# A PLE gate whose multiply moves from GpSimd in the gate stage to VectorE in the down stage (transformer block, one core)

## The chip, the core and the metric

The kernel runs on one NeuronCore of one Trainium2 chip. The metric is the device time of one execution in microseconds (us). Three executions of the kernel before took 978.75, 979.18 and 979.24 us; the median, 979.18 us, is the time that the change is measured against. The hardware profiler took one further execution of the same program; all rows below come from it.

## The reference, cut to what matters

One block on 512 tokens of width 1024, all in float32: a layer norm, a wide projection with a spatial gate and a gated recurrence, a merge, an output product `w_o` and a second layer norm that gives `h1`. The change touches what follows:

```python
hid = silu(h1 @ w_ffn_gate) * (h1 @ w_ffn_up)          # width 2816
ffn = hid @ w_ffn_down
ple = sigmoid(h1 @ w_ple_gate + b_ple_gate) * (p @ w_ple)
out = layer_norm(ALPHA * h1 + ffn + ple, ln2_g, ln2_b)
```

## The kernel before, in words

**Precision and units.** TensorE multiplies in a reduced 32-bit type, so each float32 operand is split into a high and a low part and each product is three matmuls (high x high, high x low, low x high). A unit of weights is 128 x 1024 elements (512 KB): it is loaded into a `raw` buffer by a DMA that SP issues, ScalarE casts the high part (`wh`, line 62), VectorE subtracts for the low part (`wl`, line 65). `wh` and `wl` have five buffers each, so these splits run ahead of TensorE by at most five units.

**Seven products.** The PLE gate and the up stage use a Strassen-like scheme (`strassen`, line 161): a product of 2 x 2 blocks takes seven block products instead of eight, named X, W, Z, Y, Z2, Y2 and Y3 after the accumulation they add to. It needs sums of weight blocks: t1 and t2 are added by GpSimd (line 181), t3 and t4 by accumulating DMAs that GpSimd issues (line 179); t4 is added into the buffer of t2 and read by the last product, Y3. The sums of activations come from `combine` (line 133).

**The stages around the change.** The product `p @ w_ple` is made at the very start and put into DRAM (`ple_dram`, line 412). Much later, after the second layer norm, comes the PLE gate (`pg_prod`, `pg_evac`, lines 884 to 923). For each of the four output quadrants (c11, c12, c22, c21; 256 tokens x 512 columns each) `pg_evac` loads the PLE product of that quadrant into `pl` (line 910, SP), adds the two partial results on VectorE (line 916), takes the sigmoid on ScalarE (line 918), multiplies it by `pl` on GpSimd (line 919) and stores the result back to `ple_dram` (line 920, SP). The up stage (`up`, line 931) follows: eleven groups of 256 columns, each a seven-product scheme over the gate and up weights, ending in `hid`. The down stage (lines 972 to 1031) first scales the residual in `r1` (`g1`, line 988), loads the gated PLE (`gp`, line 987), adds the bias `b1` to it (line 989) and adds the two (line 990). Then come eleven pairs of down units, `wd`, each with a split of the activations (`hidh`, `hidl`) and 48 matmuls; the last two pairs form a tail that ends one token tile after the other, and the residual is added as each accumulator is read (lines 1016 and 1024).

**What sets the order.** The code is written in Tile. A planner in the compiler simulates a timeline and from it fixes the order of the instructions on every engine's queue, in which earlier program text has priority among what is ready. On the chip each queue (TensorE, VectorE, ScalarE, GpSimd, SP) runs strictly in that order: an instruction that waits holds up everything behind it on its queue, DMA issues included. So a change in one place can move instructions elsewhere. Buffers of a pool with the same tag are reused in turn, and a load into one waits for the last reader of its previous content.

Of the kernel before, what the change touches and what calls it, by code (L numbers as in the profile page):

```python
# [8 lines left out]
F32 = mybir.dt.float32  # L9
# [3 lines left out]
ALU = mybir.AluOpType  # L13

P = 128
D = 1024
KT = D // P
T = 512
TT = T // P
# [13 lines left out]
def block_kernel(  # L33
# [7 lines left out]
    nc = tc.nc  # L41
    V, S, G, PE = nc.vector, nc.scalar, nc.gpsimd, nc.tensor
# [11 lines left out]
    dram = ctx.enter_context(tc.tile_pool(name="dram", bufs=1, space=bass.MemoryType.DRAM))  # L54

    def ps_tile(name):
        return psum.tile([P, 2, 512], F32, tag="ps", name=name)
# [22 lines left out]
    def unit_b(w, k0, c0, name, **kw):  # L80
        return load_unit(
            w[k0 * P:(k0 + 2) * P, c0:c0 + 512].rearrange("(k p) c -> p k c", p=P), 2, 512, name, **kw)
# [169 lines left out]
    def load_bc(pool, vec, name, n=D, tag=None, bufs=1):  # L252
        t = pool.tile([P, n], F32, tag=tag or name, name=name, bufs=bufs)
        nc.sync.dma_start(t, row_bc(vec, n))
        return t
# [20 lines left out]
    def ln_aggr(st, mr):  # L276
        V.bn_aggr(out=mr, in_=st.rearrange("p a b -> p (a b)"))
        rsqrt(mr[:, 1:2], mr[:, 1:2], LN_EPS)
# [21 lines left out]
    hh = hpool.tile([P, KT, T], F32R, name="hh")  # L300
    hl = hpool.tile([P, KT, T], F32R, name="hl")
    ple_dram = dram.tile([P, TT, D], F32, name="ple_dram")


    hgb_cm = tc.tile_pool(name="hgb", bufs=1, side="right")
# [400 lines left out]
    for c in range(2):  # L706
# [5 lines left out]
        for a in range(2):  # L712
            o = vn[:, 2 * a:2 * a + 2, 512 * c:512 * c + 512]
            V.tensor_tensor(out=o, in0=pss[a],
                            in1=b_v[:, 512 * c:512 * c + 512].unsqueeze(1).broadcast_to([P, 2, 512]), op=ALU.add)
# [56 lines left out]
    with tc.tile_pool(name="mg", bufs=1) as mp:  # L772
# [15 lines left out]
        for m in range(KT // 2):  # L788
            residual(m)
            res = []  # L790
            for nm, off, w, ah, al in (("a", OGA, wa, yah, yal), ("b", OGB, wb, ybh, ybl)):
                psg = ps_tile(f"ps_mg{nm}{m}")
                gemm_a(psg, win, off + 256 * m, hh, hl, f"g{nm}{m}")
                sg = mp.tile([P, 2, T], F32, tag="sg", name=f"sg{nm}{m}", bufs=3)
# [18 lines left out]
    with tc.tile_pool(name="l1", bufs=1) as lp:  # L813
        bpg = load_bc(lp, b_ple_gate[0], "bpg")
        h1f = lp.tile([P, KT, T], F32, name="h1f")
        acc = [ps_tile(f"ps_wo{t}") for t in range(TT)]

        def wo_mm(t, kp, us):
            for c in range(2):
                h, l = us[c]  # L820
                for k in range(2):
                    kk = 2 * kp + k
                    mm_b(acc[t][:, c, :], t, mgh, mgl, kk, h, l, k, kk == 0, kk == KT - 1)

        def wo_tail(t):
            for c in range(2):
                for kp, us in tails:
                    h, l = us[c]
                    for k in range(2):
                        kk = 2 * kp + k  # L830
                        mm_b(acc[t][:, c, :], t, mgh, mgl, kk, h, l, k, kk == 0, kk == KT - 1)

        for kp in range(2):
            us = [unit_b(wo, 2 * kp, 512 * c, f"wo{kp}_{c}") for c in range(2)]
            for t in range(TT):
                wo_mm(t, kp, us)
        tails = [(kp, [unit_b(wo, 2 * kp, 512 * c, f"wo{kp}_{c}") for c in range(2)]) for kp in (2, 3)]

        def turn(t):
            ps = ps_tile(f"ps_h1_{t}")  # L840
            psv = ps.rearrange("p a (b c) -> p (a b) c", c=P)
            for k in range(KT):
                PE.transpose(psv[:, k, :], r1[:, t, k * P:(k + 1) * P], ident)
            f = h1f[:, :, t * P:(t + 1) * P]
            for k in range(KT):
                S.activation(f[:, k, :], psv[:, k, :], AF.Identity, scale=vecT[:, 104 + k:105 + k],
                             bias=vecT[:, 112 + k:113 + k])
            if t < 2:
                ts = slice(t * P, t * P + P)
                for n, fs in (("11", f[:, 0:4, :]), ("12", f[:, 4:8, :])):  # L850
                    split(comb[n][0][:, :, ts], comb[n][1][:, :, ts], fs)
            else:
                combine(comb, cpool, h1f, slice((t - 2) * P, (t - 1) * P))

        def norm1(t):

            r = r1[:, t, :]
            st = lp.tile([P, 2, 6], F32, tag="lnst1", name=f"lnst1_{t}", bufs=2)
            for c in range(2):
                o = r[:, 512 * c:512 * c + 512]  # L860
                V.tensor_tensor(out=o, in0=acc[t][:, c, :], in1=o, op=ALU.add)
                V.bn_stats(out=st[:, c, :], in_=o)
            mr = lp.tile([P, 3], F32, tag="mr1", name=f"mr1_{t}", bufs=2)
            ln_aggr(st, mr[:, 0:2])
            V.scalar_tensor_tensor(out=mr[:, 2:3], in0=mr[:, 0:1], scalar=-1.0, in1=mr[:, 1:2],
                                   op0=ALU.mult, op1=ALU.mult)
            S.activation(r, r, AF.Identity, scale=mr[:, 1:2], bias=mr[:, 2:3])

        for t in range(TT):
            wo_tail(t)  # L870
            if t > 1:
                turn(t - 2)
            with tc.high_priority(offset=300):
                norm1(t)
        mgpool_cm.__exit__(None, None, None)
        yapool_cm.__exit__(None, None, None)
        cpool_cm = tc.tile_pool(name="comb", bufs=1, side="right")
        cpool = cpool_cm.__enter__()
        comb.update({n: tuple(cpool.tile([P, 4, HT], F32R, name=f"c{n}{z}") for z in "hl") for n in COMB[2:]})
        with tc.tile_pool(name="pg", bufs=1, side="right") as pp:  # L880
            pch = {}
            pmid = {}

            def pg_prod(chain, units, n, first, last):
                if first:
                    pch[chain] = ps_tile(f"ps_pg{chain}")
                for t in range(2):
                    product_b(pch[chain], units, comb[n], first, last, t)
                    if n in ("11", "12") and t == 1:
                        turn(2 if n == "11" else 3)  # L890

            def pg_mid(n, x, y, op):
                pmid[n] = pp.tile([P, 2, 512], F32, name=f"pg_{n}")
                for t in range(2):
                    V.tensor_tensor(out=pmid[n][:, t, :], in0=x[:, t, :], in1=y[:, t, :], op=op)

            def pg_evac(n):
                bias = [bpg[:, 512 * c:512 * c + 512].unsqueeze(1).broadcast_to([P, 2, 512]) for c in range(2)]
                if n == "p1":

                    pg_mid("p1", pch["X"], bias[0], ALU.add)
                    pg_mid("p1c", pch["X"], bias[1], ALU.subtract)
                elif n in ("y6", "z5"):
                    pg_mid(n, pch[n[0].upper()], pmid["p1c"], ALU.subtract)
                else:
                    i, j = int(n[1]) - 1, int(n[2]) - 1
                    cs = slice(512 * j, 512 * j + 512)
                    sg = pp.tile([P, 2, 512], F32, tag="sgp", name=f"sgp{i}{j}", bufs=2)
                    pl = pp.tile([P, 2, 512], F32, tag="pl", name=f"pl{i}{j}", bufs=2)
                    nc.sync.dma_start(pl, ple_dram[:, 2 * i:2 * i + 2, cs])  # L910
                    chain, add = {"c11": ("W", "p1"), "c22": ("Y", "z5"), "c12": ("Z", "y6"), "c21": ("Y", "p1")}[n]
                    x, y = pch[chain], pmid[add]
                    if n == "c21":
                        x, y = y, x
                    for t in range(2):
                        V.tensor_tensor(out=sg[:, t, :], in0=x[:, t, :], in1=y[:, t, :],
                                        op=ALU.subtract if n == "c21" else ALU.add)
                    S.activation(sg, sg, AF.Sigmoid)
                    G.tensor_tensor(out=sg, in0=sg, in1=pl, op=ALU.mult)
                    nc.sync.dma_start(ple_dram[:, 2 * i:2 * i + 2, cs], sg)  # L920

            strassen(wx, [[src_b(wpg, 4 * a, 4, 512 * b) for b in range(2)] for a in range(2)], "pg",
                     "X W Z Y Z2 Y2 Y3", pg_prod, pg_evac)


# [46 lines left out]
    with tc.tile_pool(name="fin", bufs=1) as lp:  # L972
# [8 lines left out]
        b1 = load_bc(lp, ln1_b[0], "b1", tag="lng", bufs=2)  # L981
        S.activation(g1, g1, AF.Copy, scale=ALPHA)
        S.activation(b1, b1, AF.Copy, scale=ALPHA)
        for t in range(TT):
            r = r1[:, t, :]
            gp = lp.tile([P, D], F32, tag="gp", name=f"gp{t}", bufs=2)
            nc.sync.dma_start(gp, ple_dram[:, t, :])
            V.tensor_tensor(out=r, in0=r, in1=g1, op=ALU.mult)
            V.tensor_tensor(out=gp, in0=gp, in1=b1, op=ALU.add)
            V.tensor_tensor(out=r, in0=r, in1=gp, op=ALU.add)  # L990
        g2 = load_bc(lp, ln2_g[0], "g2", tag="lng", bufs=2)
        b2 = load_bc(lp, ln2_b[0], "b2", tag="lng", bufs=2)
        acc = [ps_tile(f"ps_d{t}") for t in range(TT)]
# [15 lines left out]
        for t in range(TT):  # L1009
            r = r1[:, t, :]  # L1010
# [17 lines left out]
            for c in range(2):  # L1028
                cs = slice(512 * c, 512 * c + 512)
# [35 lines left out]
```

## Time and profile before

| what | value |
|---|---|
| median of three executions | 979.18 us |
| the profiled execution, its time | 981.31 us |
| its span, first to last instruction | 979.6 us |
| TensorE matmuls busy | 939.3 us, 96% |
| VectorE busy | 609.7 us, 62% |
| ScalarE busy | 360.6 us, 37% |
| GpSimd busy | 247.4 us, 25% |
| mean granted TensorE clock | 0.99 of full speed |

PE is TensorE, PEld its weight load, DVE is VectorE, ACT ScalarE, POOL GpSimd, SP the engine that issues most DMAs. Times in rows are microseconds from the start of the span unless marked ns. A share of the whole span averages over stages with different limits, so rows are read by stage.

### The profile page before, as it was taken

The numbers are of one execution on the slowest core, as the hardware profiler recorded it, in microseconds if no ns is written. First come the engines' busy times: TensorE is split into PE (matmuls) and PEld (weight loads), VectorE is DVE, ScalarE is ACT, GpSimd is POOL, SyncE is SP. The second block draws the span as 40 slices with busy tenths as digits, with TensorE's granted clock in tenths as the row PEclk, the third lists the DMA queues.
The fourth block names the chain that finished last, engine by engine and source line by source line (L and its number), as shares of the span: only waits on it lengthen the run. The fifth ranks groups of instructions, "written<-read, shape, count | busy, mean of one in ns | idle before, by whom it ended". The sixth has DMA issues, their size and how long they took to land. (4 is left out here: it accounts for less than half of the span.)

```text
span 979.6 us, 13295 instructions
## 1 busy us (share of the span) xinstructions
PE 939.3 (96%) x5513; PEld 811.0 (83%) x5513; DVE 609.7 (62%) x652; ACT 360.6 (37%) x424; POOL 247.4 (25%) x159
## 2 busy tenths in 40 slices
PE   6999999999999999999999988888999999999996
PEld 4788878877888888888888866788999999988885
DVE  6758743857348664333323469867887888657317
ACT  4243322232424362222323195434444545333311
POOL 4414220405006036000000503842343242000004
PEclk9999999999999999999999998999999999999999
DMA  8442222222422633323236323976667765246212
GB/s 271 149 140 89 84 66 87 71 82 83 141 77 65 215 95 120 108 86 106 87 104 218 76 76 74 290 182 165 151 153 168 177 150 122 74 174 213 93 37 86
DMA packets 85325, 122.56 MB, mean 125 GB/s; under 512 B 3865, under 2 KB 60817, under 8 KB 85265
## 3 DMA queue, kind: packets, MB, share of 16 engines
q1 hardware_dynamic: 81520, 108.08, 34.2%
q0 software_dynamic: 3744, 13.63, 8.1%
q8 instruction: 43, 0.70, 0.3%
q14 instruction: 18, 0.14, 0.0%
HBM read 101.77 MB, written 6.29 MB: 110 GB/s over the span
## 5 line engine op out<-in xcount | busy, mean ns | idle before, releaser
L65 DVE TENSOR_TENSOR wl_f_t<-t_f,wh_f_t 128x1024 fp32r<-128x1024 f32 x33 | 72.4, 2194 | 9.3 <-ACT wh_f_t L62 9.2
L62 ACT CAST wh_f<-raw_f 128x1024 fp32r<-128x1024 f32 x41 | 43.0, 1048 | 80.6 <-PE ps_f_b L224 37.1
L101 PE MATMUL ps_d<-wh_d,hidl 128*128 128x512 f32 x172 | 66.6, 389 | 0.0
L100 PE MATMUL ps_d<-wl_d,hidh 128*128 128x512 f32 x172 | 66.6, 389 | 0.0
L99 PE MATMUL ps_d<-wh_d,hidh 128*128 128x512 f32 x172 | 66.3, 389 | 0.0
L65 DVE TENSOR_TENSOR wl_f<-raw_f,wh_f 128x1024 fp32r<-128x1024 f32 x41 | 56.2, 1370 | 15.9 <-ACT wh_f L62 15.9
L181 POOL TENSOR_TENSOR t_f<-raw_f,raw_f 128x1024 f32<-128x1024 f32 x11 | 28.9, 2631 | 111.1 <-DVE wl_f L65 100.8
L62 ACT CAST wh_f_t<-t_f 128x1024 fp32r<-128x1024 f32 x33 | 34.6, 1051 | 44.6 <-PE ps_f_b L225 17.7
L489 POOL TENSOR_TENSOR k<-sgm,lv 128x512 f32<-128x512 f32 x8 | 16.1, 2036 | 123.4 <-DVE lv L541 123.4
L267 POOL TENSOR_TENSOR mr<-mr,nhalf 128x1 f32<-128x1 f32 x12 | 10.7, 892 | 144.8 <-DVE mr L266 139.6
L181 POOL TENSOR_TENSOR t_pg<-raw_pg,raw_pg 128x1024 f32<-128x1024 f32 x2 | 4.8, 2408 | 166.9 <-DVE wl_wo L65 165.6
L62 ACT CAST wh_d<-raw_d 128x1024 fp32r<-128x1024 f32 x22 | 23.1, 1048 | 62.1 <-PE ps_d L101 30.4
L65 DVE TENSOR_TENSOR wl_d<-raw_d,wh_d 128x1024 fp32r<-128x1024 f32 x22 | 26.9, 1222 | 28.9 <-ACT wh_d L62 28.9
L100 PEld LDWEIGHTS ps_d<-wl_d,hidh 128*128 128x128 f32 x172 | 32.3, 188 | 6.6
L99 PEld LDWEIGHTS ps_d<-wh_d,hidh 128*128 128x128 f32 x172 | 32.2, 188 | 6.6
L101 PEld LDWEIGHTS ps_d<-wh_d,hidl 128*128 128x128 f32 x172 | 32.3, 188 | 6.6
L181 POOL TENSOR_TENSOR t_f<-t_f,raw_f 128x1024 f32<-128x1024 f32 x11 | 35.9, 3264 | 0.9
L65 DVE TENSOR_TENSOR wl_wb<-raw_wb,wh_wb 128x1024 fp32r<-128x1024 f32 x8 | 14.1, 1773 | 25.7 <-ACT wh_wb L62 25.7
L222 PE MATMUL ps_f_a<-c11h,wh_f 128*128 128x256 f32 x88 | 25.8, 294 | 4.1 <-ACT wh_f L62 4.1
L225 PE MATMUL ps_f_a<-c11h,wl_f 128*128 128x256 f32 x88 | 25.7, 292 | 4.1 <-DVE wl_f L65 4.1
L101 PE MATMUL ps_i<-wh_i,hl 128*128 128x512 f32 x64 | 25.8, 404 | 2.2 <-DVE hl L65 2.2
L65 DVE TENSOR_TENSOR wl_wa<-raw_wa,wh_wa 128x1024 fp32r<-128x1024 f32 x8 | 9.8, 1226 | 28.4 <-ACT wh_wa L62 28.4
(399 smaller groups left out, 3202.7 us busy)
## 6 DMA issues: line engine op xcount, KB each, us to landing
raw_f<-in_w_ffn_gate_dram SPq DMA_DIRECT2D x22, 512.0 KB
raw_f<-in_w_ffn_up_dram SPq DMA_DIRECT2D x22, 512.0 KB, 7.8
raw_d<-in_w_ffn_down_dram SPq DMA_DIRECT2D x22, 512.0 KB, 3.7
raw_f<-raw_f POOLq DMA_DIRECT2D x11, 512.0 KB, 4.7
t_f<-raw_f POOLq DMA_DIRECT2D x11, 512.0 KB, 7.2
raw_i<-in_w_in_dram SPq DMA_DIRECT2D x8, 512.0 KB, 4.5
raw_f<-in_w_in_dram SPq DMA_DIRECT2D x8, 512.0 KB
raw_q<-in_w_in_dram SPq DMA_DIRECT2D x8, 512.0 KB, 3.7
```

The costliest lines, as they stand in the source:

```text
L62: S.copy(h, src)
L65: (eng or V).tensor_tensor(out=l, in0=src, in1=h.bitcast(F32), op=ALU.subtract)
L99: PE.matmul(ps, acth[:, kk, ts], h[:, k, :], start=first, stop=False)
L100: PE.matmul(ps, acth[:, kk, ts], l[:, k, :], start=False, stop=False)
L101: PE.matmul(ps, actl[:, kk, ts], h[:, k, :], start=False, stop=last)
L181: G.tensor_tensor(out=d, in0=a, in1=b, op=ALU.add)
L222: PE.matmul(o, h[:, k, cs], ah[:, k, :], start=first and j == 0 and k == 0, stop=False, skip_group_check=True)
L225: PE.matmul(o, l[:, k, cs], ah[:, k, :], start=False, stop=last and j == 1 and k == 3, skip_group_check=True)
L267: G.tensor_tensor(out=dst, in0=dst, in1=nhalf[:, 0:n], op=ALU.pow)
L489: G.tensor_tensor(out=dst.rearrange("p n (c i) -> p n c i", i=16), in0=s4, in1=bc16(sc3), op=ALU.mult)
```

## The change

The PLE multiply leaves the gate stage. `pg_evac` no longer loads `pl`, no longer multiplies on GpSimd, and stores the bare sigmoid to a new DRAM tile, `gate_dram`, with a DMA on ScalarE's queue in place of SP's. In the down stage the bias `b1` is added to the residual directly, and for each token tile and each half of the columns the PLE product and the gate are loaded (SP), multiplied on VectorE and added to the residual. The order of the seven products is as it was.

```diff
+    gate_dram = dram.tile([P, TT, D], F32, name="gate_dram")
...
                     sg = pp.tile([P, 2, 512], F32, tag="sgp", name=f"sgp{i}{j}", bufs=2)
-                    pl = pp.tile([P, 2, 512], F32, tag="pl", name=f"pl{i}{j}", bufs=2)
-                    nc.sync.dma_start(pl, ple_dram[:, 2 * i:2 * i + 2, cs])
...
                     S.activation(sg, sg, AF.Sigmoid)
-                    G.tensor_tensor(out=sg, in0=sg, in1=pl, op=ALU.mult)
-                    nc.sync.dma_start(ple_dram[:, 2 * i:2 * i + 2, cs], sg)
+                    S.dma_start(gate_dram[:, 2 * i:2 * i + 2, cs], sg)
...
         for t in range(TT):
             r = r1[:, t, :]
-            gp = lp.tile([P, D], F32, tag="gp", name=f"gp{t}", bufs=2)
-            nc.sync.dma_start(gp, ple_dram[:, t, :])
             V.tensor_tensor(out=r, in0=r, in1=g1, op=ALU.mult)
-            V.tensor_tensor(out=gp, in0=gp, in1=b1, op=ALU.add)
-            V.tensor_tensor(out=r, in0=r, in1=gp, op=ALU.add)
+            V.tensor_tensor(out=r, in0=r, in1=b1, op=ALU.add)
+            for c in range(2):
+                cs = slice(512 * c, 512 * c + 512)
+                gp = lp.tile([P, 512], F32, tag="gp", name=f"gp{t}{c}", bufs=2)
+                nc.sync.dma_start(gp, ple_dram[:, t, cs])
+                sg = lp.tile([P, 512], F32, tag="sgd", name=f"sgd{t}{c}", bufs=2)
+                nc.sync.dma_start(sg, gate_dram[:, t, cs])
+                V.tensor_tensor(out=gp, in0=gp, in1=sg, op=ALU.mult)
+                V.tensor_tensor(out=r[:, cs], in0=r[:, cs], in1=gp, op=ALU.add)
```

## Rows read from the trace of the kernel before

**Rows 1.** Windows: busy time of each engine, granted clock (PEclk), DMA share by stage.

```profile
core 0: us, PE busy (x) PEld busy (x) DVE busy (x) ACT busy (x) POOL busy (x), PEclk, DMA share, GB/s
580.00:604.00 24.00, 18.75 (x72) 14.01 (x71) 21.27 (x30) 17.95 (x32) 7.25 (x1) 0.86 0.00 1
617.70:637.90 20.20, 15.95 (x97) 14.43 (x95) 20.06 (x14) 8.78 (x9) 20.04 (x10) 0.92 1.00 287
670.00:968.00 298.00, 298.00 (x2082) 277.93 (x2081) 208.94 (x205) 116.57 (x129) 65.22 (x39) 1.00 0.50 135
```

**Rows 2.** Timeline of PE: start, us, line, tiles; idle before and what ended it.

```profile
620.62 0.39 PE L225 MATMUL ps_f_a<-c11h,wl_f 128*128 128x256 f32 x1 [2.50 <-DVE wl_f L65]
...
637.90 0.38 PE L222 MATMUL ps_f_a<-ca3h,wh_f 128*128 128x256 f32 x1 [1.74 <-DVE z L948]
...
645.16 0.38 PE L222 MATMUL ps_f_a<-c11h,wh_f 128*128 128x256 f32 x1 [1.54 <-ACT wh_f L62]
...
647.21 0.38 PE L225 MATMUL ps_f_a<-c11h,wl_f 128*128 128x256 f32 x1 [1.55 <-DVE wl_f L65]
...
666.47 0.58 PE L222 MATMUL ps_f_a<-c11h,wh_f 128*128 128x256 f32 x1 [2.57 <-ACT wh_f L62]
```

**Rows 3.** Windows, the two stretches of low granted clock (columns as in rows 1).

```profile
621.60:625.00 3.40, 3.40 (x18) 3.40 (x17) 3.40 (x3) 1.04 (x1) 3.40 (x3) 0.50 1.12 331
665.90:669.30 3.40, 2.83 (x13) 2.84 (x14) 3.40 (x6) 1.46 (x2) 0.68 (x1) 0.51 0.33 116
```

**Rows 4.** Timeline of POOL, gate and early up stage.

```profile
596.75 7.53 POOL L919 TENSOR_TENSOR sgp<-sgp,pl 128x1024 f32<-128x1024 f32 x1 [20.05 <-ACT sgp L918]
604.22 1.79 POOL L179 DMA_DIRECT2D t_pg<-raw_pg  x2
616.41 3.07 POOL L181 TENSOR_TENSOR t_f<-raw_f,raw_f 128x1024 f32<-128x1024 f32 x1 [10.39 <-DMA raw_f<-in_w_ffn_up_dram]
...
633.37 2.79 POOL L919 TENSOR_TENSOR sgp<-sgp,pl 128x1024 f32<-128x1024 f32 x1
636.11 0.87 POOL L179 DMA_DIRECT2D t_f<-raw_f  x1
```

**Rows 5.** Timeline of DVE, gate and early up stage.

```profile
597.84 1.22 DVE L65 TENSOR_TENSOR wl_pg_t<-t_pg,wh_pg_t 128x1024 fp32r<-128x1024 f32 x1
...
618.36 2.21 DVE L65 TENSOR_TENSOR wl_f<-raw_f,wh_f 128x1024 fp32r<-128x1024 f32 x1
```

**Rows 6.** Timeline of SP, its DMA issues in the gate stage.

```profile
604.31 0.36 SPq L920 DMA_DIRECT2D ple_dram<-sgp  x1
...
605.29 1.42 SPq L170 DMA_DIRECT2D raw_f<-in_w_ffn_up_dram  x2
```

**Rows 7.** Timeline of DVE in the down stage.

```profile
873.43 4.63 DVE L988 TENSOR_TENSOR r<-r,g 128x1024 f32<-128x1024 f32 x4 [1.70 <-ACT g L982]
...
882.52 1.22 DVE L65 TENSOR_TENSOR wl_d<-raw_d,wh_d 128x1024 fp32r<-128x1024 f32 x1
...
884.80 1.22 DVE L65 TENSOR_TENSOR wl_d<-raw_d,wh_d 128x1024 fp32r<-128x1024 f32 x1
...
888.20 1.22 DVE L65 TENSOR_TENSOR wl_d<-raw_d,wh_d 128x1024 fp32r<-128x1024 f32 x1
...
893.26 2.50 DVE L989 TENSOR_TENSOR gp<-gp,b 128x1024 f32<-128x1024 f32 x2 [1.57 <-DMA gp<-ple_dram]
...
916.71 1.23 DVE L65 TENSOR_TENSOR wl_d<-raw_d,wh_d 128x1024 fp32r<-128x1024 f32 x1 [7.38 <-ACT wh_d L62]
...
927.59 1.23 DVE L65 TENSOR_TENSOR wl_d<-raw_d,wh_d 128x1024 fp32r<-128x1024 f32 x1 [7.38 <-ACT wh_d L62]
...
949.62 0.69 DVE L1016 TENSOR_TENSOR r<-ps_d,r 128x512 f32<-128x512 f32 x1 [9.93 <-PE ps_d L101]
```

**Rows 8.** Timeline of ACT, early up stage.

```profile
643.11 1.05 ACT L62 CAST wh_f_t<-t_f 128x1024 fp32r<-128x1024 f32 x1 [6.87 <-DMA t_f<-raw_f]
```

**Rows 9.** Tile ple_dram: its DMA issues (ns) and all their times to landing.

```profile
L920 SPq DMA_DIRECT2D ple_dram<-sgp x4: 360/366/367, 604.3 to 639.5; - x4
...
DMA to landing us min/median/max: 4.7/5.3/5.9
```

## The prediction, made before the change was run

> **What bounds the kernel now.** I cut the span into stages first and looked at how busy each engine is in each [rows 1]. From 670 us to 968 us TensorE is busy without a gap, in the later up stage and, from about 843, in the down stage, at a granted clock of 1.00: there only work that makes TensorE late can cost, and nothing that frees another engine can help. The stretch from 617.7 to 637.9 is different: TensorE is busy 15.95 of 20.20 us, while VectorE (20.06) and GpSimd (20.04) have no gap and the DMA share is 1.00. That is the end of the PLE gate and the start of the up stage, where the change takes work away.
>
> The second view is TensorE in order of time, for the gaps it shows there [rows 2]: 2.50, 1.74, 1.54, 1.55 and 2.57 us, 9.90 in all. After the first and the last gap the granted clock stands at 0.50 (1.2 GHz of 2.4) for 3.4 us [rows 3]; what was done there at half rate would take 1.7 us at 1.00, so the two low stretches cost 2 x 1.7 = 3.4 us. The addressable loss is 9.9 + 3.4 = **13.3 us**.
>
> The third view follows these gaps to GpSimd and the DMA queues. GpSimd multiplies the first quadrant (c11) by the PLE product for 7.53 us and only then, at 604.22, issues the two accumulating DMAs that make t4 [rows 4], although VectorE had finished with t2, the last thing they waited for, at 597.84 + 1.22 = 599.06 [rows 5]. SP holds the c11 store in its order, and so every load behind it, until 604.31; the first two up loads leave at 605.29 [rows 6]. The DMA engines were idle from 580 to 604 (share 0.00) and full afterwards [rows 1]. GpSimd's next sum, t_f, began at 616.41 [rows 4] and the split of the first up unit, beside it, took 2.21 us at 618.36 [rows 5], where a split alone takes 1.22 [rows 7]: that split ends the 2.50 us gap. Later c22's multiply (633.37, 2.79 us) stands ahead of the DMA for the next t4 (636.11) [rows 4]; ScalarE waits 6.87 us for its landing [rows 8], and TensorE's gaps of 1.54 and 1.55 us come right after.
>
> **The change part by part.**
>
> Removed from GpSimd: four multiplies, 7.53 and three like the one of 2.79 [rows 4], some 15.9 us. Two have an effect, the one ahead of 604.22 and the one ahead of 636.11. The t4 DMAs can go about 5 us earlier (599.06 against 604.22), into idle DMA engines; the second t4 goes at least 2.8 us earlier.
>
> Removed from SP: four loads of pl (L910) and four stores (L920). With the store off its queue the first up load no longer waits for GpSimd: it takes the buffer of a gate unit whose split follows the one at 597.84 [rows 5], so it can go at about 600, some 5 us earlier. GpSimd's t_f sums, then, no longer stand beside the split that TensorE waits for. I take the 2.50 us gap and its 1.7 us of clock as gone: **-4.2**. The gaps of 1.54 and 1.55 need the second t4 3.1 us earlier; it gets 2.8 from one multiply alone and more from the earlier start of GpSimd's queue: **-3.1**. The 1.74 us gap waits for VectorE's z, behind a split beside the third and fourth multiplies; without the stretch of 2.21 - 1.22 = 1.0 us it shrinks by **-1.0**. The last gap, 2.57 us at 666.47 with its 1.7 of clock, is 33 us after the multiply of 633.37; nothing I can follow ties it to them, so it stays: 0, with 4.3 as the other bound. Sum **-8.3**, bounds 0 and -13.3.
>
> The Trainium skill, page "SBUF — State Buffer", section "SBUF: two separate sides", calls the port pair of VectorE and GpSimd an exclusive lock that the loser waits out whole. The rows agree as far as they go: a 2.21 us split beside GpSimd's sum, 1.22 alone, and a multiply of 7.53 us against 2.79 beside a busy VectorE. By that rule each removed multiply could return up to its 2.8 us to VectorE, 1.8 more than the 1.0 I count for z; the sum would be 10.1 in place of 8.3 and the time about 971.
>
> Added to ScalarE: four stores (L918, then the DMA on ScalarE's own queue). No row shows a DMA issued there. The nearest are 0.36 us for SP's issue [rows 6] and 0.87 for GpSimd's [rows 4], and the issue must wait for the sigmoid, about 1.05 us long like a cast of that size [rows 8]. Bounds: 0 and 4 x 1.9 = 7.7 us of ScalarE's time. Behind each store stand casts for the next units, for which TensorE waits. ScalarE is busy 8.78 of 20.20 us in this stretch [rows 1], and the fourth store falls into the 6.87 us wait; I take 0 on the path. If that cover went, up to 1.9 us per store would come back. The two sgp buffers are still freed by stores that land about 5.9 us after their issue [rows 9], earlier than before.
>
> Added to the down stage: twice the bytes are read back there (gp and gate in 16 loads of 256 KB, against gp alone in 4 of 512 KB), and VectorE's residual chain grows. Before: 4 scalings (4.63 us [rows 7]), 4 bias adds and 4 PLE adds of the same shape, 3 x 4.63 = 13.9 us. After: 4 scalings, 4 bias adds, and 8 multiplies and 8 adds of half size, which I count as 8 whole ones: 4 x 4.63 = 18.5 us, so +4.6. In most of the stage this lies beside matmuls: a pair of down units takes TensorE 927.59 - 916.71 = 10.88 us and VectorE three splits of 1.22 [rows 7]. The tight place is pair 3. Pair 8 ends at 949.62 [rows 7], so pair 3 begins at 949.62 - 6 x 10.88 = 884.3 and needs its second unit six matmuls (1.4 us) later, at 885.7; the split at 882.52 gives it at 883.7. There are 2.0 us to spare. The bias adds no longer wait for a load, so they can follow the scalings at once: that puts eight operations ahead of this split where six stood, 2.3 us more, and costs 0.3 us. With all eight and two chunks of multiply and add (2.3 us) first, then a split of the activations and the first unit's own, that unit would be ready at 873.43 + 9.3 + 2.3 + 1.2 + 1.2 = 887.4, 3.1 us late. Bounds 0.3 and 3.1; I take the middle, near the order with one chunk: **+1.7**. Of gp and sgd there are two half-size buffers each, so SP comes to four rounds of loads instead of two, each waiting for VectorE's add, with weight loads behind. A round's landing is 4.7 to 5.9 us [rows 9]; VectorE waited 1.57 us for one [rows 7]. Pair 4 begins at 895.2; its splits end at 884.80 + 1.22 = 886.0 and 889.4 [rows 7], 9 and 7 us ahead, and I cost these waits at nothing; they are a rival below.
>
> The end (normalisation, stores) is untouched. The profiled execution took 981.31 us (span 979.6), 2.1 above the median of 979.18; I apply the difference to the median: 979.2 - 8.3 + 1.7 = **972.6 us**.
>
> **Rivals.**
>
> *More goes (17%).* The last gap was the tail of the same lateness. Then all 13.3 us go, and with the cheap order in the down stage the time is 979.2 - 13.3 + 0.3 = 966.2. For it: no gap after 670. Against: that gap's cast waited for a buffer that TensorE frees.
>
> *The DMA engines are the limit, so about the same (14%).* The share is 1.00 between 617.7 and 637.9 at 287 GB/s [rows 1]. If stores and loads merely change places there, only the two pl loads of that stretch, 1.05 MB, leave it: 1.05 MB / 287 GB/s = 3.7 us. With the dear order in the down stage: 979.2 - 3.7 + 3.1 = 978.6. Against it: the engines idled until 604, so early transfers find room. The Trainium skill, page "DMA: Bandwidth & Descriptors", section "Issuing engines are not separate DMA queues", says that transfers started by different engines share the same 16 DMA engines and that starting them elsewhere saves only the issuing time. By that rule the new queue brings no bandwidth, and this rival would be the result; the idle stretch before 604 speaks for a gain from order all the same.
>
> *The rounds of loads starve the down stage, so slower (17%).* Place: VectorE between 885 and 915, in order, with multiplies that wait for gp and sgd ahead of splits. Each round costs some 1.5 us of issue and up to 5.9 of landing; three rounds waited out are about 22 us, against 9 us of lead and some 7 us free per pair. The point from which it decides is when these waits pass that lead: TensorE then stands, and its clock drops as it did after the gaps of 2.5 us. Price 3.1 + 1.7 + about 3 = 7.8; with only the first gap gained (4.2) the time is 979.2 - 4.2 + 7.8 = 982.8. For it: the 1.57 us wait and the halved buffers. Against: 124 us of down stage in which lateness can be made up.
>
> *Nothing that matters moves (3%).* The planner orders every engine's instructions from a simulated timeline; it may put the t4 DMAs behind something else. Then 979.
>
> **How the numbers follow.** My forecast has 49%. A measurement of this kernel can tell about 0.2%, 2.0 us, from no change. Faster: 49 + 17 = 66%; same: 14 + 3 = 17%; slower: 17%. The range of 966 to 982 us reaches from the case in which all gaps go to just short of the starved down stage; the forecast's own range is 968 to 976.
>
> **What would show it.** Right: t4's DMAs near 599, up loads near 600 to 604, no TensorE gap at the first up unit, no low clock near 622, the next t4 cast without its 6.87 us wait; in the down stage one TensorE gap of at most some 3 us near pair 3. Wrong: TensorE gaps of the old size between 617 and 650 with other releasers (then the DMA engines or VectorE were the limit), ScalarE casts late behind its own stores, or several gaps between 885 and 915 ended by down splits.

## The result, and the profile after

| | median us | runs | ratio to before, 95% interval |
|---|---|---|---|
| before | 979.21 | 978.75 to 979.95 (4) | |
| changed | 966.86 | 965.70 to 968.67 (4) | 0.9875 [0.9858, 0.9892] |

The changed kernel is 12.35 us faster. The forecast was 972.6, 6.6 us faster; the time lies in its range, beside the rival "more goes" (966.2). Timed again (e10 below), the same kernel gave 965.6 us against 979.22, ratio 0.9859 [0.9842, 0.9875].

First the stages, in windows shifted by the time that TensorE had gained there; columns as in [rows 1].

```profile
578.00:601.50 23.50, 18.87 (x71) 14.28 (x72) 21.43 (x31) 17.71 (x30) 1.77 (x2) 0.85 0.29 64
614.70:634.90 20.20, 19.09 (x140) 17.83 (x140) 14.87 (x15) 10.70 (x11) 8.05 (x5) 1.00 0.89 244
654.00:952.00 298.00, 298.00 (x2083) 278.02 (x2083) 214.41 (x216) 116.83 (x129) 65.96 (x39) 1.00 0.53 142
```

In the middle stretch TensorE stands 1.11 us where it stood 4.25, GpSimd is busy 8.05 us of 20.20 where it had no gap, VectorE 14.87, and the clock is 1.00. The DMA engines work before 601 (share 0.29 against 0.00) and are no longer full after it. The last stretch is as gapless as before, the down stage included.

TensorE's waits from 600 us to its last matmul (total, times, longest) are one line; the five gaps of [rows 2] and both low stretches of [rows 3] are gone.

```profile
PE ps_pgY L237 <- DVE sgp L915: 1.1, 1, 1.1
```

GpSimd, SP and VectorE in order of time, answering [rows 4 to 6]; the planner's order is otherwise much the same here.

```profile
594.55 0.89 POOL L179 DMA_DIRECT2D t_pg<-raw_pg  x1 [20.32 <-DVE wl_pg_t L65]
596.96 0.88 POOL L179 DMA_DIRECT2D t_pg<-raw_pg  x1 [1.51 <-DVE wl_pg_t L65]
605.15 2.40 POOL L181 TENSOR_TENSOR t_f<-raw_f,raw_f 128x1024 f32<-128x1024 f32 x1 [7.32 <-DMA raw_f<-in_w_ffn_up_dram]
...
621.57 0.85 POOL L179 DMA_DIRECT2D t_f<-raw_f  x1 [0.64 <-DVE wl_f_t L65]
```

```profile
597.80 2.48 SPq L170 DMA_DIRECT2D raw_f<-in_w_ffn_up_dram  x2
```

```profile
613.11 1.21 DVE L65 TENSOR_TENSOR wl_f<-raw_f,wh_f 128x1024 fp32r<-128x1024 f32 x1
...
617.82 1.27 DVE L915 TENSOR_TENSOR sgp<-ps_pgY,pg_z 128x512 f32<-128x512 f32 x2
```

Each profile counts from its own start, and the changed kernel's reaches the first gate product 2.46 us sooner, before any code that was changed (see below). With that taken off, the first t4 DMA leaves 7.2 us earlier (594.55 against 604.22), the up loads 5.0 us, GpSimd's first up sum 8.8 us and the second t4 (621.57) 12.1 us. The split of the first up unit takes 1.21 us, alone. The one new gap: c22's sum (617.82) stands on VectorE behind a split that waits for its cast, and Y3 may not overwrite what that sum reads.

ScalarE's new DMA issues cost it 0.37 us each: a store right behind its sigmoid, then the casts of 614.77, the first of which the split ahead of c22's sum waits for. Before the next t4 cast (629.73) ScalarE waits 1.54 us where it waited 6.87 [rows 8].

```profile
594.24 0.38 ACTq L918 DMA_DIRECT2D gate_dram<-sgp  x1
...
614.31 0.37 ACTq L918 DMA_DIRECT2D gate_dram<-sgp  x1
614.77 2.00 ACT L62 CAST wh_f_t<-t_f 128x1024 fp32r<-128x1024 f32 x2 [0.49 <-ACT sgp L917]
...
629.73 1.05 ACT L62 CAST wh_f_t<-t_f 128x1024 fp32r<-128x1024 f32 x1 [1.54 <-DMA t_f<-raw_f]
```

VectorE in the down stage, answering [rows 7]:

```profile
857.39 4.63 DVE L984 TENSOR_TENSOR r<-r,g 128x1024 f32<-128x1024 f32 x4 [1.28 <-ACT g L980]
861.94 1.22 DVE L65 TENSOR_TENSOR hidl<-hid,hidh 128x1024 fp32r<-128x1024 f32 x1
863.08 0.68 DVE L992 TENSOR_TENSOR gp<-gp,sgd 128x512 f32<-128x512 f32 x1
863.68 1.22 DVE L65 TENSOR_TENSOR wl_d<-raw_d,wh_d 128x1024 fp32r<-128x1024 f32 x1
864.81 2.35 DVE L985 TENSOR_TENSOR r<-r,b 128x1024 f32<-128x1024 f32 x2
867.08 0.68 DVE L992 TENSOR_TENSOR gp<-gp,sgd 128x512 f32<-128x512 f32 x1
867.69 1.22 DVE L985 TENSOR_TENSOR r<-r,b 128x1024 f32<-128x1024 f32 x1
868.82 1.22 DVE L65 TENSOR_TENSOR wl_d<-raw_d,wh_d 128x1024 fp32r<-128x1024 f32 x1
...
892.96 1.34 DVE L992 TENSOR_TENSOR gp<-gp,sgd 128x512 f32<-128x512 f32 x2 [4.18 <-DMA gp<-ple_dram]
...
934.00 0.69 DVE L1019 TENSOR_TENSOR r<-ps_d,r 128x512 f32<-128x512 f32 x1 [9.93 <-PE ps_d L101]
```

The planner put only three bias adds and two half multiplies between the scalings and pair 3's second split. Pair 3 begins at 934.00 - 65.3 = 868.7 and needs that split at 870.1; it ends at 868.82 + 1.22 = 870.0. By this count the 2.0 us to spare are used up to the last tenth; the trace has no wait of TensorE there.

**How the spans compare.** The profiled spans differ by 15.6 us (979.6 and 964.0), the medians by 12.35. Most of the difference between the two is the start: the first gate product runs at 572.98 before and at 570.52 after, and nothing ahead of it was changed. To leave that out, the table below measures from that product to the first matmul of the last accumulator (`ps_last`); by it the change is worth 395.5 - 382.3 = 13.2 us. By the gaps: 13.3 gone, 1.1 new, and a gap before 600 that shrank from 1.04 to 0.64, make 12.6. The shrinking is not the edit's: the same gap is 1.20 us long in the changed kernel's second profile.

### The profile page after: what moved, and what is told of

It reads as the page before. It is cut to its first block, busy times and chain, and to the rows that moved or that the text cites. A ratio compares the mean times of both kernels' runs of the same rounds, so it can differ in the third digit from the quotient of the medians.

```text
span 964.0 us, 13316 instructions
## 1 busy us (share of the span) xinstructions
PE 934.2 (97%) x5513; PEld 807.3 (84%) x5513; DVE 606.3 (63%) x664; ACT 361.2 (37%) x424; POOL 230.5 (24%) x155
## 4 chain that ended last, share of the span: by engine, by line
PE 85%; DVE 7%; ACT 2%; POOL 2%; issue 1%; DMA 1%; SPq 0%; DVEq 0%; POOLq 0%; ACTq 0%
PE ps_f_b L225 4%; PE ps_f_b L222 4%; PE ps_f_b L224 4%; PE ps_d L101 4%; PE ps_d L100 4%; PE ps_d L99 4%; PE ps_f_a L225 3%; PE ps_f_a L222 3%; PE ps_f_a L224 3%; PE ps_mwa L94 2%; PE ps_mwa L95 2%; PE ps_mwa L93 2%; PE ps_f L93 2%; PE ps_mgb L94 2%; PE ps_f L94 2%; PE ps_gu L93 2%
## 5 line engine op out<-in xcount | busy, mean ns | idle before, releaser
L65 DVE TENSOR_TENSOR wl_f<-raw_f,wh_f 128x1024 fp32r<-128x1024 f32 x41 | 49.7, 1213 | 15.8 <-ACT wh_f L62 15.8
L181 POOL TENSOR_TENSOR t_f<-raw_f,raw_f 128x1024 f32<-128x1024 f32 x11 | 26.4, 2398 | 112.4 <-DVE wl_f L65 105.1
L62 ACT CAST wh_f_t<-t_f 128x1024 fp32r<-128x1024 f32 x33 | 34.6, 1052 | 36.9 <-PE ps_f_b L225 16.3
L953 DVE TENSOR_TENSOR g<-p,ps_f_b 128x512 f32<-128x512 f32 x11 | 7.6, 687 | 30.2 <-PE ps_f_b L225 30.2
L65 DVE TENSOR_TENSOR wl_wo<-raw_wo,wh_wo 128x1024 fp32r<-128x1024 f32 x8 | 9.8, 1223 | 25.8 <-ACT wh_wo L62 25.8
```

Source lines behind the costliest of these rows:

```text
L62: S.copy(h, src)
L65: (eng or V).tensor_tensor(out=l, in0=src, in1=h.bitcast(F32), op=ALU.subtract)
L181: G.tensor_tensor(out=d, in0=a, in1=b, op=ALU.add)
```

## The experiments

All against the kernel before on the same chip. "Stretch" is the time from the first gate product to `ps_last` in the run's own profile; the changed kernel's two profiles give 382.3 and 382.8.

| run | median us | ratio, 95% interval | stretch us |
|---|---|---|---|
| before | 979.2 to 979.5 | | 395.5 |
| changed | 966.86 | 0.9875 [0.9858, 0.9892] | 382.3 |
| e1, unused multiply on GpSimd | 970.77 | 0.9909 [0.9894, 0.9924] | 386.1 |
| e2, gate stores on SP | 966.65 | 0.9865 [0.9851, 0.9880] | 382.8 |
| e3, unused PLE loads | 967.80 | 0.9872 [0.9856, 0.9889] | 382.6 |
| e4, before, stores on GpSimd | 976.24 | 0.9965 [0.9952, 0.9978] | 394.0 |
| e8, before, SP free of GpSimd | 973.36 | 0.9934 [0.9920, 0.9949] | 388.8 |
| e5, before, multiplies on VectorE | 968.42 | 0.9885 [0.9869, 0.9902] | 384.1 |
| e7, one buffer in the down stage | 966.29 | 0.9870 [0.9855, 0.9884] | 382.5 |
| e10, changed again | 965.60 | 0.9859 [0.9842, 0.9875] | 382.8 |
| e9, other order of products | 971.39 | 0.9917 [0.9902, 0.9932] | 388.1 |

The theory after the first result: the multiplies cost nothing themselves; what stood behind them did, the t4 DMAs and the up sums on GpSimd's queue. Rival one: the store on SP's queue was the cause. Rival two: the DMA engines were the limit.

**e1: GpSimd's time put back, and nothing else.** The changed kernel with

```diff
                     S.dma_start(gate_dram[:, 2 * i:2 * i + 2, cs], sg)
+                    du = pp.tile([P, 2, 512], F32, tag="du", name=f"du{i}{j}", bufs=2)
+                    G.tensor_tensor(out=du, in0=sg, in1=sg, op=ALU.mult)
```

> The changed kernel, and behind each of the four sigmoids an unused multiply of the same size on GpSimd (gate by itself into a scratch tile). No load, no store and no wait of another queue comes back, only GpSimd's time and its place ahead of the t4 DMAs and the up sums. Theory (GpSimd's queue held t4 and the sums back): most of the 12.3 us is lost again, 973 to 979 us, with the TensorE gaps of 2.5, 1.5 and 1.55 us and the low clock back between 615 and 650. Rival one (SP's queue, held by the store, was the cause) and rival two (the DMA engines were the limit): 966 to 968 us, no gap.

Measured: 970.77 us, 3.9 above the changed kernel: a third of the gain, not most of it. GpSimd's order of time shows the mechanism:

```profile
596.94 7.00 POOL L920 TENSOR_TENSOR du<-sgp 128x1024 f32<-128x1024 f32 x1 [20.03 <-ACT sgp L917]
603.89 1.79 POOL L179 DMA_DIRECT2D t_pg<-raw_pg  x2
605.07 3.05 POOL L181 TENSOR_TENSOR t_f<-raw_f,raw_f 128x1024 f32<-128x1024 f32 x1
```

and the waits of TensorE between 600 and 700 its price:

```profile
PE ps_f_b L222 <- DVE u L957: 1.3, 1, 1.3
PE ps_f_a L225 <- DVE wl_f L65: 0.9, 1, 0.9
PE ps_pgY L237 <- DVE sgp L915: 0.8, 1, 0.8
PE ps_f_a L222 <- ACT wh_f L62: 0.3, 1, 0.3
PE ps_f_a L222 <- DVE z L948: 0.2, 1, 0.2
```

Counted from each run's first gate product, the t4 DMAs are held back again (30.7 us after it; 31.2 before, 24.0 changed), but the first up sum is not (31.9; 43.4 before, 34.6 changed), since the up load was not held. The 2.5 us gap does not come back. Neither the theory nor rival one holds alone.

**e2: the store on SP's queue.** `S.dma_start` becomes `nc.sync.dma_start` for the gate store.

> The changed kernel with the four gate stores issued by SP in place of ScalarE. They wait only for a sigmoid, not for GpSimd. Theory: 966 to 969 us, since the store is ready at about 594 and nothing behind it on SP can leave before 598 anyway. Rival one, in the form that any store on SP's queue holds the up loads: 970 us or more, first up loads later than 600 and the TensorE gap at the first up unit back.

Measured: 966.65 us, no difference from ScalarE's queue. A store on SP that waits for a sigmoid holds nothing that matters; what counts is what it waits for. The Trainium skill, page "DMA: Bandwidth & Descriptors", section "Issuing engines are not separate DMA queues", says that the choice of engine saves only issuing time, and for the queue as such this pair of runs agrees.

**e3: the traffic put back.** The changed kernel with the load of `pl` in `pg_evac`, into a tile that nothing reads.

```diff
+                    pl = pp.tile([P, 2, 512], F32, tag="pl", name=f"pl{i}{j}", bufs=2)
+                    nc.sync.dma_start(pl, ple_dram[:, 2 * i:2 * i + 2, cs])
```

> The changed kernel with the four loads of the PLE product put back on SP in the gate stage, unused: 2 MB more traffic there, two of the loads on the full DMA engines after 600. Theory: 966 to 969 us. Rival two (the DMA engines were the limit, 1.05 MB at 287 GB/s is 3.7 us): 970 to 971 us.

Measured: 967.80 us with an interval that covers the changed kernel's ratio; the stretch is 0.3 us longer. But the edit does not put the traffic where the rival wants it. Nothing reads the tile, so no load waits, and SP issues all four ahead of the gate's work:

```profile
571.09 5.61 SPq L911 DMA_DIRECT2D pl<-ple_dram  x4
```

They land within 6.9 us, well ahead of the full stretch after 600. So this run does not test rival two; e5 does.

**e4: the store off SP, the multiply kept.** The kernel before with

```diff
-                    nc.sync.dma_start(ple_dram[:, 2 * i:2 * i + 2, cs], sg)
+                    G.dma_start(ple_dram[:, 2 * i:2 * i + 2, cs], sg)
```

> The kernel before with its four stores issued by GpSimd, behind its own multiply, in place of SP. SP's queue holds no store, so the up loads can leave at about 600 as in the changed kernel; the multiplies stay, ahead of the t4 DMAs. Theory: GpSimd's order still delays t4 and the sums, 975 to 980 us. Rival one: 967 to 970 us, as the up loads are free.

Measured: 976.24 us, in the theory's range, but the trace shows that the edit did not set SP free. SP's first issues of the stage, and GpSimd's multiply:

```profile
602.76 0.36 SPq L910 DMA_DIRECT2D pl<-ple_dram  x1
603.23 0.96 SPq L170 DMA_DIRECT2D raw_f<-in_w_ffn_up_dram  x2
```

```profile
594.08 8.65 POOL L919 TENSOR_TENSOR sgp<-sgp,pl 128x1024 f32<-128x1024 f32 x1 [20.04 <-ACT sgp L918]
```

The third PLE load takes the buffer that the first multiply reads, so it waits for the same 602.73 and holds the up loads in the store's place. TensorE's gaps after 600 still sum to 9.6 us, against 9.9 before. The run can't tell the theories apart; e8 was made to.

**e8: SP free of every wait for GpSimd.** As e4, with a buffer for each PLE load.

```diff
-                    pl = pp.tile([P, 2, 512], F32, tag="pl", name=f"pl{i}{j}", bufs=2)
+                    pl = pp.tile([P, 2, 512], F32, tag="pl", name=f"pl{i}{j}", bufs=4)
```

> The kernel before with SP's queue free of every wait for GpSimd: the four stores are issued by GpSimd and the four PLE loads have a buffer each, so none waits for a multiply. GpSimd's multiplies stay. If the 12.3 us come from two causes, GpSimd's own time (3.9 us by the run with the unused multiply) and SP's queue held by the store and the third load, this gives 979.2 - 8.4 = 971 us, within 969 to 973. If GpSimd's order is nearly all of it, 975 to 978 us. If SP's queue is all of it, 967 us.

Measured: 973.36 us: 6.1 us gained with the multiplies in place. That is 2.4 us short of the two causes added up and just outside that range; it also misses GpSimd's order alone, by 1.6 us, and SP's queue alone, by 6.4. The edit does two things more: the stores' issues now stand on GpSimd's queue, and the third and fourth PLE load leave before 570, out of the full stretch. The up loads leave early,

```profile
597.91 10.18 SPq L170 DMA_DIRECT2D raw_f<-in_w_ffn_up_dram  x2
```

and what is left is GpSimd's share; TensorE's waits from 600 to 700 of more than 0.5 us:

```profile
PE ps_pgZ L239 <- DVE ca3l L65: 2.0, 1, 2.0
PE ps_f_a L222 <- DVE z L948: 1.8, 1, 1.8
PE ps_f_a L225 <- DVE wl_f L65: 1.0, 1, 1.0
PE ps_f_a L222 <- ACT wh_f L62: 0.7, 1, 0.7
```

The longest ends with a split on VectorE, which for this shape took 0.69 us at 591.35 and takes 4.46 here, while GpSimd's sum runs from 604.95 for 3.02 us:

```profile
604.07 4.46 DVE L65 TENSOR_TENSOR ca3l<-h1f,ca3h 128x512 fp32r<-128x512 f32 x1
```

**e5: the multiply on VectorE, all else as before.** `G.tensor_tensor` becomes `V.tensor_tensor` in line 919.

> The kernel before with the four multiplies on VectorE in place of GpSimd; loads, stores and the down stage as before. SP's store and loads then wait for VectorE, which does the multiply in about 1.2 us where it stands in its order. Theory (both GpSimd's time and SP's hold are gone, 4 x 1.2 us of VectorE come in): 967 to 971 us. Rival (what counts is that the multiply leaves the gate stage altogether): 974 us or more.

Measured: 968.42 us. Taking the multiply off GpSimd, in one word of the code, gives 11 of the 12.35 us. What the move to the down stage adds, 1.6 us, is not clear of noise, as the two intervals overlap; e5's stretch is 1.3 to 1.8 us longer than the changed kernel's two. The planner's order changed too: the up loads (599.69) now go ahead of the store (601.52). The longest wait is the one that the changed kernel has, with a multiply of 1.22 us (615.38) ahead of the sum on VectorE; in the profiles without that multiply it is 1.0 to 1.7 us:

```profile
PE ps_pgY L237 <- DVE sgp L916: 2.6, 1, 2.6
```

This run also settles rival two. All PLE loads and stores stay in the stage, two loads (602.21 and 617.05) and all four stores after 600, and the DMA share from 616 to 636 is 1.00 as before, yet the 11 us come:

```profile
617.05 0.46 SPq L910 DMA_DIRECT2D pl<-ple_dram  x1
```

```profile
616.00:636.00 20.00, 17.39 (x125) 16.18 (x124) 18.51 (x17) 9.77 (x11) 8.50 (x5) 1.00 1.00 266
```

**e7: the down stage squeezed.** The changed kernel with `bufs=1` for gp and sgd.

> The changed kernel with one buffer each for the gp and gate halves in the down stage in place of two: eight rounds of loads, each waiting for the add before it, so about twice the waiting on VectorE between the down splits. In the changed kernel VectorE waited 6.4 us in three rounds and TensorE nothing. Theory (the down stage has room for lateness): 966 to 969 us. Rival (the rounds of loads starve TensorE): a gap ended by a down split between 868 and 915, 971 us or more.

Measured: 966.29 us. VectorE's waits from 850 to 935 rise from 6.4 us in three to 14.5 in six, and TensorE has no wait between 660 and 955:

```profile
DVE gp L992 <- DMA gp<-ple_dram: 14.5, 6, 4.8
```

The starving rival falls with room to spare.

**e10 and e9: a try for more.** e10 is the changed kernel again. e9 changes one string in it, the order of the gate's products:

```diff
-                     "X W Z Y Z2 Y2 Y3", pg_prod, pg_evac)
+                     "X W Y Z Y2 Z2 Y3", pg_prod, pg_evac)
```

> The changed kernel as it is, timed again in the same call as the next run, as its yardstick: 966 to 968 us, with the TensorE gap of about 1.1 us before the gate's last product (waiting for VectorE's sum of c22) and none between 620 and 955.

> The changed kernel with the gate's products in the order X W Y Z Y2 Z2 Y3 in place of X W Z Y Z2 Y2 Y3: two products that add to the same accumulator never follow each other, so VectorE's sum of c22 has a whole product (5.5 us) before Y3 overwrites what it reads. Theory: the gap of 1.1 to 1.7 us before Y3 goes, 965 to 966 us. Rival (the activations' combine, not the order, sets the pace, and Y first meets its operands later than Z did): the gaps between 585 and 597 grow and the time is 968 us or more.

Measured: 965.60 and 971.39 us; e9 loses 5.8. The planner placed Z2 ahead of Y2 all the same, so the gap before Y3 stayed, and new ones came, at 604.78 and 607.01. The rival's time came with them, but not from its place: the gaps between 585 and 597 sum to 3.4 us, against 3.1 in the changed kernel. TensorE's waits in e9 after 600:

```profile
PE ps_pgZ L238 <- DVE wl_pg L65: 1.8, 1, 1.8
PE ps_pgZ L237 <- DVE pg_z L896: 1.7, 1, 1.7
PE ps_pgY L237 <- DVE sgp L915: 1.0, 1, 1.0
```

```profile
594.28 7.47 POOL L181 TENSOR_TENSOR t_f<-raw_f,raw_f 128x1024 f32<-128x1024 f32 x1 [2.38 <-DVE wl_pg_t L65]
```

In this order GpSimd's up sum fell into a run of VectorE's work without a gap and took 7.47 us in place of 2.40. That the gaps at 604 and 607 come from it was not tried by itself. No version here is clearly faster than the changed kernel.

## Why the prediction was right, and where it was short

The mechanism was right: the gain lies between 617 and 670, where GpSimd's multiply held back the t4 DMAs on its own queue and the up loads on SP's. Counted as in the profile before, the t4 DMAs left at 597.0 and 599.4 and the up loads at 600.3, where it had said 599 and 600. Of the sum, in its own terms:

- **The 2.50 us gap and its clock (-4.2)**: gone, as said. What set the split free was the up load, 5.0 us earlier, as the prediction had it, so that the sum no longer stood beside it. The step named the store as what held SP; e4 shows that the third PLE load held it just as long. Both left with the change.
- **The gaps of 1.54 and 1.55 (-3.1)**: gone, as said; the second t4 leaves 12.1 us earlier, where the prediction asked for 3.1 and counted on at least 2.8.
- **The 1.74 us gap (-1.0)**: gone whole, 0.7 more. The split ahead of z was earlier and not merely shorter.
- **The last gap (0, bound 4.3)**: this is the step that failed, "nothing I can follow ties it to them". It went with its low clock, 4.3 us. Lines of the trace before show what it waited for: t4's DMA of the second group among the DMA issues of 652 to 656 (last column: us from issue to landing), and ScalarE in order of time, with the cast that reads t4 and, behind it, the cast whose end at 666.41 ends the gap.

```profile
t_f<-raw_f POOLq DMA_DIRECT2D x1, 512.0 KB, 9.4
```

```profile
663.90 1.04 ACT L62 CAST wh_f_t<-t_f 128x1024 fp32r<-128x1024 f32 x1 [3.90 <-PE ps_f_a L225]
...
665.38 1.03 ACT L62 CAST wh_f<-raw_f 128x1024 fp32r<-128x1024 f32 x1
```

Issued at 654.43, the DMA landed 9.4 us later, at 663.8, and the cast began at 663.90. The same DMA a group later took 7.0. The prediction read the wait by the releaser named, a matmul that ended at 663.90 too. In the changed kernel the same cast goes as soon as its DMA has landed, and ahead of that matmul:

```profile
648.40 1.06 ACT L62 CAST wh_f_t<-t_f 128x1024 fp32r<-128x1024 f32 x1 [0.18 <-DMA t_f<-raw_f]
```

So the DMA was what counted. What made it land late is open, and that the multiplies did it is not shown: e4 keeps all four, with the up loads held, and there the same DMA takes 7.2 us and TensorE has no gap after 646. That this gap went is in part luck.

- **ScalarE's stores (0)**: nearly. They take 0.37 us each, but one (614.31) stands ahead of the casts of 614.77. From the sigmoid's start to those casts it is 1.55 us, and 0.96 in e2, which has the store on SP: some 0.6 us on the chain that ends the new gap of 1.1. e2 is no faster all the same.
- **The down stage (+1.7)**: 0. The lower bound of 0.3 had the right amount of work ahead of pair 3's second split, eight operations' worth: four scalings, three bias adds and two half multiplies, where it assumed four bias adds. What made 0 of 0.3 is that the scalings began 0.4 us earlier, counted from the end of pair 8 (934.00 - 857.39 = 76.6 us ahead of it, against 949.62 - 873.43 = 76.2). The middle of the bounds was too dear: no whole chunk came ahead.
- **Not in the sum**: the new gap of 1.1 us before Y3, a wait that takes the place of the old ones.

13.3 - 1.1 + 0.4 = 12.6 against 12.35 measured and 13.2 in the stretch. The miss of 5.7 us is the last gap (4.3), z (0.7) and the down stage (1.7), less the new gap (1.1), to about 0.1.

Of the rivals, "more goes" came out in its number, 966.2: all 13.3 us went, the down stage cost 0 in place of its 0.3, and the new gap 1.1. Its reason, that the last gap was the tail of the same lateness, is not shown. The DMA engines fell to e5, the starved down stage to e7. How the gain divides the runs tell only roughly: with the multiplies kept, freeing SP gives 6.1 us (e8); with SP free, GpSimd's multiplies cost 3.9 (e1, one operand, no store) to 6.5 (e8 against the changed kernel, with the stores' issues on GpSimd too). The Trainium skill's rule of the exclusive port pair, page "SBUF — State Buffer", section "SBUF: two separate sides", would have given about 971 by the prediction's estimate. The traces agree that the two engines stretch each other's work: 7.00 and 8.65 us for a multiply beside VectorE's run of splits, and 4.46 us for a split of 0.69 in e8. How the price divides between this and what queued behind GpSimd was not separated.

## What to carry to other kernels

On an in-order queue, price an instruction by what stands behind it and for what it waits, on every queue that waits with it: freeing SP of the stores and loads that waited for GpSimd's multiplies gained 6.1 us (e8), and multiplies with no such wait behind them cost 3.9 us (e1). When an engine's name ends a wait, check when the DMAs that feed the same instruction landed before calling the wait unrelated. Look in the trace whether an edit did what it was meant to: e3's loads left too early to test anything, and e4 did not free SP. And try the smallest edit first: moving the multiply to VectorE in place gave 11 of 12.35 us.

## What the runs showed of the hardware that was not expected

The granted clock's low stretches differ between executions of one program. The changed kernel's two profiles, the same windows, columns as in [rows 1]; first the earlier run, then the later:

```profile
571.40:574.60 3.20, 2.94 (x17) 2.60 (x18) 2.72 (x7) 3.20 (x8) 1.39 (x1) 1.00 0.00 0
```

```profile
571.40:574.60 3.20, 3.13 (x12) 2.84 (x13) 2.73 (x7) 3.20 (x9) 1.40 (x1) 0.50 0.00 0
```

At these gaps the later run fell to 0.50 and the first did not. The start varies likewise: the profile before stood at 0.50 between 38 and 41 us, as e3 did (e1: 0.55), and these three reached the first gate product at 573.0 to 573.4; the other eight, the changed kernel's two among them, stood at 1.00 there and reached it at 570.3 to 571.0. A single pair of profiles can so be 2 to 3 us apart in code that is the same in both. The window of 38 to 41 us, first of the kernel before, then of the changed kernel's earlier run:

```profile
38.00:41.00 3.00, 3.00 (x8) 2.35 (x9) 2.72 (x3) 0.00 (x0) 0.13 (x1) 0.50 0.01 4
```

```profile
38.00:41.00 3.00, 3.00 (x15) 2.46 (x14) 1.85 (x3) 0.00 (x0) 1.00 (x1) 1.00 0.00 0
```
